# The opening of a two-layer decoder trunk: square sums moved to VectorE, a fourth gate block taken in, bank exchange and queue order rewritten

## The chip, the core and the metric

The kernel runs on one core of one Trainium2 chip. The metric is the device time of one execution in microseconds. The kernel before takes 2207.62 us (median of 3 runs, 2207.47 to 2208.49). In the profile PE is TensorE (PEld its weight loads), DVE is VectorE, ACT is ScalarE, POOL is GpSimd, and SP issues most DMAs. All arithmetic is float32; a product of two float32 matrices is made of three products of halves, high by high, high by low and low by high (fp32r), which is why every weight and every activation exists as a high and a low part.

## The reference

One sequence of 512 tokens, width 2048, passes two layers; the first is multi-scale retention with 8 heads, the second is latent attention. What matters here is how the first layer begins:

```python
def rmsnorm(x, g):
    xf = x.astype(jnp.float32)
    y = xf * lax.rsqrt(jnp.mean(xf * xf, axis=-1, keepdims=True) + EPS)
    return (y * g.astype(jnp.float32)).astype(x.dtype)

def reference(x, c, positions, ada_w, ada_b, norm_g, ret_w_in, ...):
    c_act = jax.nn.silu(c)
    for i in range(DEPTH):
        mod = (c_act @ ada_w[i] + ada_b[i])[:, None, :]
        shift, scale, gate = jnp.split(mod, 3, axis=-1)
        h = rmsnorm(x, norm_g[i]) * (1.0 + scale) + shift
        ...
def retention_branch(h, pos, w_in, gn_g, w_out):
    proj = h @ w_in
    q, k, v, g = jnp.split(proj, [RET_QK, 2 * RET_QK, 2 * RET_QK + RET_WIDTH], axis=-1)
```

So before any projection the kernel needs the sum of squares of each token (for the norm) and, for each block of 128 rows of h, two rows of matrix-vector products of silu(c) with ada_w (shift and scale). For each head of the first layer, q and k are 256 columns wide, v and the gate g are 512 columns wide.

## The kernel before, in words

Activations are kept transposed: hT has 16 blocks of 128 rows (128 of the width) by 512 tokens. The **opening** (lines 310 to 610) makes hT block by block and, while it does, already forms the products of head 0 with each block as it appears: q/k (four PSUM banks), v (four banks) and three of the four 128-column blocks of the gate g (three banks). A "unit" u is two blocks, 2u and 2u + 1; there are eight units.

The opening starts with x: eight tiles of two blocks are loaded, then squared (`square`, L456; ACT for even tiles, DVE for odd ones), folded to one block (`fold`, L466) and summed over the partitions by PE with a column of ones (`add_squares`, L469), 36 products of 128x1. `rsqrt` (L126) makes four columns of factors with one small DVE and one POOL instruction, `spread_one` (L499) spreads them over the partitions with a diagonal matrix and PE, and `normalise` (L504) multiplies x by them on DVE, straight from PSUM. silu(c) is spread over the partitions into c_all (L448).

For each block, two tiles of 1 MB of ada_w (`load_mod`, L336) are multiplied by c_all and summed along the row on DVE (`sum_mod`, L347, a 128x2048 instruction; for block 0 in two halves, L353). `make_first` (L363) turns the two sums into shift and scale on ACT and makes hT: the high part, a float copy (both ACT) and the low part (DVE). Weights are loaded by `first_load` (L319) and made into high (ACT) and low (DVE) parts.

v and q/k share one set of four PSUM banks (`acc`), so in each unit they are exchanged once: `swap` (L371) has ACT copy the four partial sums of the one out to SBUF and the four of the other back in. In an even unit PE forms q/k products for both blocks, then g, then (after the exchange) v; in an odd unit v first, then g, then q/k. `products` (L383) goes through a block by part and bank, `bank_products` (L396) through the second kind bank by bank.

The order on each engine is written out by hand: `queued` (L415) puts what it calls behind the last instruction written so far on ACT, DVE, PE and SP each. What is written without `queued` is bound only by its data and buffers. The weights and sums for unit u + 1 are prepared by `prepare_ahead` (L536, written ahead of unit u's products) and, for the odd block, by `prepare_behind` (L555, written behind the exchange). Buffers: four tiles for ada_w rows (`aw`), three for raw weights, three pairs for high and low weights, four `k4b` tiles that hold the squares first and the parts of g later, six `tmp` tiles.

In the last unit the rotary tables (`rotary_tables`, L251: a load of the positions, 17 DVE instructions, two Sin on ACT) are made: eight of its nine pieces are queued before the products, the rest behind the last exchange (L604); they are written to memory by POOL.

Behind the opening the work is a list of steps (L859 to L873), each with a load, a preparation (ACT and DVE), products and what follows them. First come two steps for block 3 of head 0's gate ("g03", 48 products), then for heads 1 to 5 eight steps of q/k and sixteen steps of v and g (`heads_steps`, L817, seven products instead of eight), for heads 6 and 7 only v and g. `sums` names the sums of hT (`form_sums`, L634) that a step forms beside its products; all eight must exist before head 1's v and g. `rows` says how many later modulation rows a step loads and sums beside. Stores of head 0's q/k and g are `keep_rows` (L616, called at L1903 to L1906).

Of the kernel before, what the change touches and what calls it, by code (L numbers as in the profile page):

```python
# [9 lines left out]
F32 = mybir.dt.float32  # L10
# [39 lines left out]
def hybrid_trunk_kernel(  # L50
# [247 lines left out]
    def qk_parts(h, u):  # L298
# [13 lines left out]
        "g": (3, lambda w, kt, b: (w_block(w, kt % 2, b), act_row(hT[kt]))),  # L312
# [6 lines left out]
    def first_load(kind, u):  # L319

        cn = 384 if kind == "g" else 512
# [25 lines left out]
    def sum_mod(kt, s):  # L347

        aw, n = mods[kt, s], 2 if kt == 0 else 1
        col = small(f"mc_{kt}_{s}", n)  # L350
        for j in range(n):
            cols = slice(j * D // n, (j + 1) * D // n)
            DVE.scalar_tensor_tensor(  # L353
                out=aw[:, cols], in0=aw[:, cols], scalar=1.0, in1=c_all[:, cols], op0=ALU.mult, op1=ALU.mult,
                accum_out=col[:, j : j + 1],
            )
        if n == 2:
            both = small(f"mc_{kt}_{s}b")
            DVE.tensor_add(both, col[:, 0:1], col[:, 1:2])
            col = both  # L360
        mods[kt, s] = col
# [9 lines left out]
    def swap(old, new):  # L371

        if old is not None:
            partial[old] = []
            for b, ps in enumerate(banks[old]):
                keep = l0p.tile([P, T], F32, tag="part", bufs=5, name=f"part_{old}_{len(loaded)}_{b}")
                ACT.copy(keep, ps)
                partial[old].append(keep)
        banks[new] = [acc(f"{new}0_{len(loaded)}_{b}") for b in range(4)]
        for b, keep in enumerate(partial.pop(new, ())):  # L380
            ACT.copy(banks[new][b], keep)
# [48 lines left out]
    def load_mods(kt):  # L430
        for s in range(2):
            mods[kt, s] = queued(load_mod, kt, s)
# [4 lines left out]
    mods[1, 0] = queued(load_mod, 1, 0)  # L437
    load_first("qk", 0)
    mods[1, 1] = queued(load_mod, 1, 1)
# [16 lines left out]
    def square(u, j=slice(0, 2)):  # L456
# [3 lines left out]
        o, i = sq[u][:, j, :], xT[u][:, j, :]  # L460
        if u % 2 and u < NU - 1:
            DVE.tensor_mul(o, i, i)
        else:
            ACT.activation(o, i, AF.Square)

    def fold(u):  # L466
        DVE.tensor_add(sq[u][:, 0, :], sq[u][:, 0, :], sq[u][:, 1, :])

    def add_squares(u, j=0):  # L469
        for t in range(NT):  # L470
            PE.matmul(
                x_sums[:, t : t + 1], sq[u][:, j, t * P : (t + 1) * P], crow, start=u + t == 0, stop=u + j == NU,
# [6 lines left out]
    for u in range(NU - 1):  # L479
        queued(square, u)  # L480
        if u < 4:
            queued(silu, u)
        if u % 2:
            queued(fold, u - 1)
            queued(fold, u)
            queued(add_squares, u - 1)
            queued(add_squares, u)
    for j in range(2):
        queued(square, NU - 1, j)
    queued(fold, NU - 2)  # L490
    queued(add_squares, NU - 1, 0)
    queued(add_squares, NU - 2)
    queued(add_squares, NU - 1, 1)
    r_col = queued(rsqrt, x_sums[:, 0:NT], NT, 1.0 / D, "x")
    POOL.dma_start(c_d, c_all[0:1, :])
    diag = tmp("x_diag")
    x_r = aux("x_r")

    def spread_one(t):  # L499
        cols = slice(t * P, (t + 1) * P)  # L500
        ACT.activation(diag[:, cols], ident, AF.Identity, scale=r_col[:, t : t + 1])
        PE.matmul(x_r[:, cols], ones, diag[:, cols], start=True, stop=True)

    def normalise(u, j=None):  # L504
        v = xT[u] if j is None else xT[u][:, j, :]
        r = x_r.unsqueeze(1).to_broadcast([P, 2, T]) if j is None else x_r
        DVE.tensor_mul(v, v, r)
# [5 lines left out]

    queued(scaled_bias)
    queued(sum_mod, 0, 0)
    for t in range(NT):
        queued(spread_one, t)
# [1663 lines left out]
```

## Time and profile before

| what | before |
|---|---|
| median of 3 runs | 2207.62 us (2207.47 to 2208.49) |
| span of the profiled execution | 2206.5 us |
| PE busy, instructions | 2162.7 us (98%), 10232 |
| DVE busy | 1562.9 us (71%) |
| ACT busy | 1014.6 us (46%) |
| bytes read from and written to memory | 395.42 and 43.00 MB, 199 GB/s over the span |
| first product of the opening | at 36.96 us |
| first product of head 1's q/k | at 188.16 us |

The profile is of one execution. A row of the timeline is: start, duration, engine, line, operation, out<-in with shapes, count of merged instructions, and in brackets the idle time of the engine before it and what released it. A row of the groups ends with busy time and mean ns of one, then idle time and releaser. A row of the waits is: total us, times, longest. Matmuls overlap, so the duration of one (0.39 us) is longer than the distance between two starts.

### The profile page before, as it was taken

The page shows a single profiled execution, that of the slowest core. Times are in us where ns is not written, and L with a number is a line of the kernel's source. Part 1 is how long each engine was busy: PE and PEld are TensorE (multiplying, and loading weights), DVE is VectorE, ACT ScalarE, POOL GpSimd, SP SyncE. Part 2 cuts the span into 40 slices and gives each one's busy share as a digit, 9 for nine tenths or more (in the row PEclk, how much of TensorE's full clock was granted, in tenths as well). Part 3 has the DMA queues.
Part 4 walks back from the last instruction along what each step waited for, and adds up shares of the span by engine and source line. Part 5 has one row for each costly group of instructions (what it writes and reads, how often), then busy time and mean ns, then how long its engine had stood idle before and what let it go on. Part 6 is the DMA issues. An engine that isn't in the chain of part 4 may idle for free.

```text
span 2206.5 us, 27730 instructions
## 1 busy us (share of the span) xinstructions
PE 2162.7 (98%) x10232; PEld 1806.3 (82%) x10232; DVE 1562.9 (71%) x2313; ACT 1014.6 (46%) x1547; POOL 101.9 (5%) x175
## 2 busy tenths in 40 slices
PE   7999999999999999999999999999999999999997
PEld 5777888888888877888888888888888889888887
DVE  5988866767676798866676776658877677766545
ACT  4764443434343444434343535434444366664443
POOL 0001000000001000000000000010000000000000
PEclk9999999999999999999999999999999999999999
DMA  7974686776868688674655556443458723235333
GB/s 302 354 275 164 195 283 223 232 251 198 277 198 268 210 283 276 203 242 141 209 189 179 191 171 215 155 157 120 145 199 293 275 90 94 85 105 180 111 104 134
DMA packets 207052, 440.26 MB, mean 200 GB/s; under 512 B 19346, under 2 KB 60338, under 8 KB 203074
## 3 DMA queue, kind: packets, MB, share of 16 engines
q1 hardware_dynamic: 194704, 399.30, 54.8%
q0 software_dynamic: 11920, 38.91, 4.5%
q8 instruction: 80, 1.31, 0.3%
q14 instruction: 58, 0.47, 0.1%
q10 hardware_dynamic: 290, 0.27, 0.0%
HBM read 395.42 MB, written 43.00 MB: 199 GB/s over the span
## 4 chain that ended last, share of the span: by engine, by line
PE 80%; DVE 8%; issue 4%; ACT 4%; DMA 2%; POOL 0%; SPq 0%; DVEq 0%; POOLq 0%; ACTq 0%
PE o L1191 13%; PE qk L163 4%; PE qk L162 4%; PE qk L161 4%; PE o L2047 4%; PE x L737 2%; PE y L737 2%; PE y L738 2%; PE y L736 2%; PE x L738 2%; PE s L737 2%; PE s L738 2%; PE x L736 2%; PE s L736 2%; PE g L161 2%
## 5 line engine op out<-in xcount | busy, mean ns | idle before, releaser
L1191 PE MATMUL o<-o_h,o_whi 128*128 128x512 f32 (+1 forms) x496 | 192.2, 388 | 0.0
L1191 PE MATMUL o<-o_h,o_wlo 128*128 128x512 f32 (+1 forms) x496 | 191.4, 386 | 0.0
L1191 PE MATMUL o<-o_l,o_whi 128*128 128x512 f32 (+1 forms) x496 | 191.3, 386 | 0.0
L163 PE MATMUL qk<-hT,qk_l 128*128 128x512 f32 x448 | 174.9, 390 | 0.4 <-DVE qk_l L136 0.4
L161 PE MATMUL qk<-hT,qk_h 128*128 128x512 f32 x448 | 174.5, 390 | 0.0
L162 PE MATMUL qk<-hT,qk_h 128*128 128x512 f32 x448 | 174.4, 389 | 0.0
L136 DVE TENSOR_TENSOR o_wlo<-o_r,o_whi 128x1024 fp32r<-128x1024 f32 x61 | 74.6, 1222 | 80.2 <-ACT o_whi L135 80.2
L136 DVE TENSOR_TENSOR qk_l<-qk_r,qk_h 128x1024 fp32r<-128x1024 f32 x56 | 68.1, 1223 | 62.4 <-ACT qk_h L135 62.1
L1191 PEld LDWEIGHTS o<-o_h,o_wlo 128*128 128x128 f32 x496 | 93.2, 188 | 18.8
L1191 PEld LDWEIGHTS o<-o_l,o_whi 128*128 128x128 f32 x496 | 93.2, 188 | 18.2
L1191 PEld LDWEIGHTS o<-o_h,o_whi 128*128 128x128 f32 x496 | 93.2, 188 | 18.2
L163 PEld LDWEIGHTS qk<-hT,qk_l 128*128 128x128 f32 x448 | 84.1, 188 | 19.4 <-DVE qk_l L136 2.1
L161 PEld LDWEIGHTS qk<-hT,qk_h 128*128 128x128 f32 x448 | 84.1, 188 | 17.5
L162 PEld LDWEIGHTS qk<-hT,qk_h 128*128 128x128 f32 x448 | 84.1, 188 | 17.5
L135 ACT CAST qk_h<-qk_r 128x1024 fp32r<-128x1024 f32 x56 | 57.8, 1049 | 85.6 <-PE qk L162 57.3
L161 PE MATMUL g<-h,g_h 128*128 128x512 f32 x232 | 90.6, 390 | 0.3 <-ACT g_h L135 0.3
L893 DVE SCALAR_TENSOR_TENSOR mod<-mod,c_bm 128x1024 f32<-128x1024 f32 x64 | 78.1, 1220 | 18.0 <-DMA mod<-in_ada_t_dram 18.0
L162 PE MATMUL g<-h,g_h 128*128 128x512 f32 x232 | 90.3, 389 | 0.0
L163 PE MATMUL g<-h,g_l 128*128 128x512 f32 x232 | 89.8, 389 | 0.0
L353 DVE SCALAR_TENSOR_TENSOR aw<-aw,c_all 128x2048 f32<-128x2048 f32 (+1 forms) x34 | 72.7, 2160 | 0.0
L135 ACT CAST o_whi<-o_r 128x1024 fp32r<-128x1024 f32 x61 | 63.5, 1052 | 19.6 <-issue 10.0
L136 DVE TENSOR_TENSOR o_w_lo<-o_w_raw,o_w_hi 128x1024 fp32r<-128x1024 f32 x32 | 38.9, 1220 | 39.4 <-ACT o_w_hi L135 39.4
(1260 smaller groups left out, 6014.3 us busy)
## 6 DMA issues: line engine op xcount, KB each, us to landing
mod<-in_ada_t_dram SPq DMA_DIRECT2D x128, 512.0 KB, 5.8
o_r<-in_ret_w_out_dram SPq DMA_DIRECT2D x64, 512.0 KB, 4.3
aw<-in_ada_t_dram SPq DMA_DIRECT2D x30, 1024.0 KB, 7.4
qk_r<-in_ret_w_in_dram SPq DMA_DIRECT2D x112, 256.0 KB, 3.9
g_r<-in_mla_w_in_dram SPq DMA_DIRECT2D x32, 512.0 KB, 4.6
o_w_raw<-in_mla_w_out_dram SPq DMA_DIRECT2D x32, 512.0 KB, 3.7
qk_d<-qk_st POOLq DMA_DIRECT2D x32, 256.0 KB, 3.5
qk_r<-qk_d SPq DMA_DIRECT2D x32, 256.0 KB, 6.2
```

The lines of the kernel that those rows point to most:

```text
L135: ACT.copy(hi, src)
L136: DVE.tensor_sub(lo, src, hi.bitcast(F32))
L161: PE.matmul(o, lhs[0], rhs[0], start=first and not seeded, stop=False, skip_group_check=seeded)
L162: PE.matmul(o, lhs[0], rhs[1], start=False, stop=False, skip_group_check=seeded)
L163: return PE.matmul(o, lhs[1], rhs[0], start=False, stop=last, skip_group_check=seeded)
L353: DVE.scalar_tensor_tensor(out=aw[:, cols], in0=aw[:, cols], scalar=1.0, in1=c_all[:, cols], op0=ALU.mult, op1=ALU.mult, accum_out=col[:, ...
L736: PE.matmul(banks[b], a[0], w[0], start=first, stop=False, skip_group_check=True)
L737: PE.matmul(banks[b], a[0], w[1], start=False, stop=False, skip_group_check=True)
L738: PE.matmul(banks[b], a[1], w[0], start=False, stop=True, skip_group_check=True)
L893: DVE.scalar_tensor_tensor(out=aw, in0=aw, scalar=1.0, in1=silu_c[j], op0=ALU.mult, op1=ALU.mult, accum_out=mc[:, j, b : b + 1],)
L1191: PE.matmul(o, w[i][:, ki, c0 + b * P : c0 + (b + 1) * P], a[j], start=first and i + j == 0, stop=last and i == 1, skip_group_check=True,)
L2047: PE.matmul(banks2[b][:, cols], w[0][i][:, 0, b * P : (b + 1) * P], o2_moving(w, u, cols)[j], start=u + i + j == 0, stop=u == KD - 1 and i ...
```

## The change

- **Squares**: ACT squares all tiles; DVE adds the squares of tiles 1 to 5 to those of tile 0 as they come (`gather`), then folds; tiles 6 and 7 are gathered into one block of their own. PE sums two blocks: 8 products instead of 36.
- **Factors**: two of the four diagonals are made on DVE; x_r is also copied to SBUF (`near`), and all but the first block are normalised from there. The sums for block 0 are queued by halves (`sum_part`) around the spread.
- **Gate**: all four blocks of head 0's gate are formed in the opening (four banks, 512 columns a load); the "g03" steps are gone.
- **Exchange**: `swap` is written bank by bank, out and back in turn; in units 1 to 7 `prepare` (one function instead of two) is written behind it, with the normalising and three sums ahead of the weights. The loads of a unit are ordered three ada_w tiles, weights, fourth ada_w tile, g, other weights. In the last unit `hand_over` copies v out and q/k in, bank by bank; all pieces of the rotary tables are written behind it, without `queued`.
- **Steps**: q/k of head 1, then q/k of head 2, then v and g of head 1, then v and g of head 2; from head 3 on as before. The sums of hT are spread over the sixteen q/k steps.

```diff
-        "g": (3, lambda w, kt, b: (w_block(w, kt % 2, b), act_row(hT[kt]))),
+        "g": (4, lambda w, kt, b: (w_block(w, kt % 2, b), act_row(hT[kt]))),
...
-        cn = 384 if kind == "g" else 512
+        cn = 512
...
+    def sum_part(kt, s, j):
+
+        if j == 0:
+            mods[kt, s] = mods[kt, s], small(f"mc_{kt}_{s}", 2)
+        aw, col = mods[kt, s]
+        cols = slice(j * D // 2, (j + 1) * D // 2)
+        DVE.scalar_tensor_tensor(
+            out=aw[:, cols], in0=aw[:, cols], scalar=1.0, in1=c_all[:, cols], op0=ALU.mult, op1=ALU.mult,
+            accum_out=col[:, j : j + 1],
+        )
+        if j == 1:
+            mods[kt, s] = small(f"mc_{kt}_{s}b")
+            DVE.tensor_add(mods[kt, s], col[:, 0:1], col[:, 1:2])
...
     def swap(old, new):
...
+        old_banks, back = banks.get(old, [None] * 4), partial.pop(new, [None] * 4)
+        partial[old], banks[new] = [], []
+        for b in range(4):
+            if old is not None:
                 keep = l0p.tile([P, T], F32, tag="part", bufs=5, name=f"part_{old}_{len(loaded)}_{b}")
-                ACT.copy(keep, ps)
+                ACT.copy(keep, old_banks[b])
                 partial[old].append(keep)
+            banks[new].append(acc(f"{new}0_{len(loaded)}_{b}"))
+            if back[b] is not None:
+                ACT.copy(banks[new][b], back[b])
+
+    def hand_over():
+
+        back, old_banks = partial.pop("qk"), banks["v"]
+        banks["qk"] = []
+        for b in range(4):
+            st = tmp(f"v0_st{b}")
+            ACT.copy(st, old_banks[b])
+            POOL.dma_start(v_d[b * P : (b + 1) * P, :], st)
+            banks["qk"].append(acc(f"qk0_{len(loaded)}_{b}"))
+            ACT.copy(banks["qk"][b], back[b])
...
+        ACT.activation(sq[u][:, j, :], xT[u][:, j, :], AF.Square)
+
+    def gather(to, u, j=None):
+        o, i = (sq[to], sq[u]) if j is None else (sq[to][:, 0, :], sq[u][:, j, :])
+        DVE.tensor_add(o, o, i)
...
+    silus = {1: 0, 2: 1, 4: 2, 5: 3}
+    for u in range(NU - 2):
         queued(square, u)
+        if u in silus:
+            queued(silu, silus[u])
+        if u > 0:
+            queued(gather, 0, u)
+    queued(square, NU - 2)
     for j in range(2):
         queued(square, NU - 1, j)
+    queued(gather, 0, 0, 1)
+    queued(add_squares, 0, True, False)
+    queued(gather, NU - 2, NU - 2, 1)
+    for j in range(2):
+        queued(gather, NU - 2, NU - 1, j)
+    queued(add_squares, NU - 2, False, True)
...
     queued(scaled_bias)
+    queued(sum_part, 0, 0, 0)
+    r_col = queued(rsqrt, x_sums[:, 0:NT], NT, 1.0 / D, "x")
...
     for t in range(NT):
         queued(spread_one, t)
+    low_v = queued(prepares["v", 0])
+    queued(sum_part, 0, 0, 1)
+    queued(sum_part, 0, 1, 0)
     queued(normalise, 0, 0)
+    queued(ACT.copy, near, x_r)
+    queued(sum_part, 0, 1, 1)
     low = queued(make_first, 0)
     queued(low_v)
+    low_g = queued(prepares["g", 0])
+    queued(low_g)
     queued(low)
...
     def load_unit(u):
         here, there = ("qk", "v") if u % 2 == 0 else ("v", "qk")
+        load_mods(2 * u)
+        load_mods(2 * u + 1, (0,))
         load_first(here, u)
+        load_mods(2 * u + 1, (1,))
         load_first("g", u)
         load_first(there, u)
...
+    def prepare(u):
         here, there = ("qk", "v") if u % 2 == 0 else ("v", "qk")
+        queued(normalise, u)
+        for s in range(2):
+            queued(sum_mod, 2 * u, s)
+        queued(sum_mod, 2 * u + 1, 0)
+        low_here = queued(prepares[here, u])
+        queued(low_here)
+        low = queued(make_first, 2 * u)
+        queued(sum_mod, 2 * u + 1, 1)
         queued(low)
+        low_g, low_there = (queued(prepares[kind, u]) for kind in ("g", there))
         low = queued(make_first, 2 * u + 1)
+        for fn in (low_g, low_there, low):
+            queued(fn)
...
     swap(None, "v")
     queued(products, "v", 0)
+    queued(sum_mod, 1, 0)
+    banks["g"] = [aux(f"g0_{b}") for b in range(4)]
     queued(products, "g", 0)
+    queued(queued(prepares["qk", 0]))
+    queued(normalise, 0, 1)
     queued(swap, "v", "qk")
+    queued(sum_mod, 1, 1)
     low = queued(make_first, 1)
+    queued(low)
     queued(products, "qk", 0)
-    prepare_ahead(1, low)
     queued(products, "qk", 1)
     queued(products, "g", 1)
     queued(swap, "qk", "v")
-    low = prepare_behind(1)
+    prepare(1)
     queued(products, "v", 1)
...
-            prepare_ahead(u + 1, low)
-        else:
-            queued(low)
-            for _ in range(8):
-                queued(next, tables)
...
         if more:
             queued(swap, here, there)
-            low = prepare_behind(u + 1)
+            prepare(u + 1)
         else:
+            queued(hand_over)
             for _ in tables:
                 pass
...
+    steps = qk_steps(1, sums=lambda u: {1: 0, 2: 1, 4: 2, 5: 3, 6: 4}.get(u))
+    steps += qk_steps(2, rows=lambda u: 1, sums=lambda u: {0: 5, 2: 6, 4: 7}.get(u))
     for h in range(1, RH):
+        if 2 < h < 6:
+            steps += qk_steps(h, rows=lambda u: 1)
         steps += heads_steps(h)
...
-    for b in range(3):
+    for b in range(4):
         queued(keep_rows, g0[b], g_d, b * P, f"g0_st{b}", AF.Silu, tmp)
```

`qk_steps` makes the same eight steps as the plain q/k steps before.

137 lines of the change are left out of this document (33 added, 104 removed).

## The prediction

> **What bounds the kernel now.** I read the windows first (columns: stretch, length, busy time and count of PE, PEld, DVE, ACT, POOL, then granted TensorE clock, DMA share, GB/s), cut at the first product of the opening and at the first product of the q/k step of head 1.
>
> ```profile
> 0.00:36.96 36.96, 24.69 (x88) 19.70 (x89) 15.22 (x26) 13.88 (x21) 4.36 (x11) 1.00 0.71 270
> 36.96:188.16 151.20, 138.52 (x577) 110.35 (x578) 127.02 (x135) 99.42 (x166) 7.03 (x13) 0.97 0.83 303
> 188.16:300.00 111.84, 111.29 (x483) 89.97 (x482) 93.75 (x133) 48.77 (x62) 2.67 (x5) 1.00 0.61 195
> ```
>
> From 188.16 on PE is idle for 0.55 us in 111.84: there only the number of matmuls counts, and the change leaves that number alone. All that can be won lies before 188.16. The middle stretch holds the opening's 16 x 33 = 528 products and the 48 of gate block 3: 576, and 577 are counted. What a product costs when nothing is waited for, and what a unit (two row blocks of h, 66 products) waits for, is in the timeline:
>
> ```profile
> 113.16 1.07 PE L392 MATMUL qk<-hT,qk_wlo 128*128 128x512 f32 x4
> ...
> 117.69 4.24 PE L392 MATMUL g<-hT,g_k4b 128*128 128x512 f32 x18
> 118.14 0.39 ACT L367 ACTIVATE a_col<-mc,bias,vcol 128x1 f32<-128x1 f32 x1 [4.44 <-DVE aw L353]
> ...
> 119.99 0.82 ACT L330 CAST g_k4b<-g_raw 128x768 fp32r<-128x768 f32 x1
> ...
> 121.67 0.57 ACT L377 COPY part_qk<-qk 128x512 f32<-128x512 f32 x1
> ...
> 122.91 0.50 PE L392 MATMUL v<-v_whi,hT 128*128 128x512 f32 x1 [0.98 <-ACT v L381]
> ```
>
> Between 113.16 and 117.69 PE starts 20 products: 0.2265 us each. So 576 need 130.5 us and got 151.20: **20.7 us are lost** between 36.96 and 188.16, beside the 36.96 before. The other rows show how a unit loses its part: ACT waits 4.44 us for a sum on DVE, then makes hT, casts g and the next weights, and only then reaches the bank exchange (121.67), so that PE has run out of g products and waits for the first bank at 122.91. One unit, and PE's waits grouped:
>
> ```profile
> 99.56:115.81 16.25, 15.27 (x68) 12.31 (x67) 14.51 (x15) 11.46 (x19) 0.00 (x0) 1.00 0.95 344
> ```
>
> ```profile
> PE v L392 <- ACT v L381: 8.9, 4, 5.9
> ...
> PE qk L392 <- ACT qk L381: 2.6, 3, 1.0
> ```
>
> A unit takes 16.25 us where 66 x 0.2265 = 14.95 are PE's: ACT and DVE waiting for each other set the pace, each of them with time to spare (DVE 14.51, ACT 11.46 busy). One exchange waited 5.9 us.
>
> **The start.** First the squares, their sums on PE, the factors, and the first product.
>
> ```profile
> 6.08 1.23 DVE L462 TENSOR_TENSOR x_sq<-x 128x1024 f32<-128x1024 f32 x1 [5.06 <-DMA x<-in_x_t_dram]
> ...
> 8.94 1.23 DVE L462 TENSOR_TENSOR x_sq<-x 128x1024 f32<-128x1024 f32 x1 [0.44 <-DMA x<-in_x_t_dram]
> ...
> 12.04 15.52 PE L471 MATMUL x_sums<-ones,x_sq 128*128 128x1 f32 x72
> ...
> 27.84 2.03 POOL L131 TENSOR_TENSOR x_r<-x_v,mhalf 128x4 f32<-128x4 f32 x1 [14.28 <-DVE bias L510]
> ...
> 30.36 2.08 PE L502 MATMUL x_r<-x_diag,ones 128*128 128x128 f32 x8 [2.80 <-ACT x_diag L501]
> ...
> 32.47 0.69 DVE L507 TENSOR_TENSOR x<-x,x_r 128x512 f32<-128x512 f32 x1 [2.15 <-PE x_r L502]
> ...
> 36.96 2.08 PE L392 MATMUL v<-v_whi,hT 128*128 128x512 f32 x4 [4.53 <-ACT hT L243]
> 38.83 1.79 PE L392 MATMUL v<-v_wlo,hT 128*128 128x512 f32 x4
> ```
>
> ```profile
> L353 DVE SCALAR_TENSOR_TENSOR aw<-aw,c_all 128x2048 f32<-128x2048 f32 x30 | 67.9, 2285 | 0.0
> L332 DVE TENSOR_TENSOR v_wlo<-v_raw,v_whi 128x1024 fp32r<-128x1024 f32 x8 | 9.8, 1224 | 1.3 <-ACT v_whi L330 1.2
> ...
> L507 DVE TENSOR_TENSOR x<-x,x_r 128x1024 f32<-128x1024 f32 x7 | 8.5, 1215 | 0.0
> L332 DVE TENSOR_TENSOR g_k4b<-g_raw,g_k4b 128x768 fp32r<-128x768 f32 x8 | 7.7, 958 | 0.0
> L353 DVE SCALAR_TENSOR_TENSOR aw<-aw,c_all 128x1024 f32<-128x1024 f32 x4 | 4.7, 1220 | 0.0
> L467 DVE TENSOR_TENSOR x_sq<-x_sq 128x512 f32<-128x512 f32 x7 | 4.6, 686 | 0.5 <-ACT x_sq L464 0.4
> ```
>
> ```profile
> L243 ACT ACTIVATE hT<-x,b_col,a_col 128x512 fp32r<-128x512 f32 x16 | 13.1, 816 | 0.5
> L381 ACT COPY v<-part_v 128x512 f32<-128x512 f32 x16 | 9.5, 591 | 0.5
> ...
> L330 ACT CAST v_whi<-v_raw 128x1024 fp32r<-128x1024 f32 x8 | 8.4, 1047 | 0.1
> ...
> L464 ACT ACTIVATE x_sq<-x 128x1024 f32<-128x1024 f32 x4 | 4.2, 1054 | 5.0 <-PE x_sums L471 3.6 <-DMA x<-in_x_t_dram 1.4
> ...
> L449 ACT ACT_TABLE_LOAD x1 | 1.3, 1283 | 0.0
> ```
>
> Before, 36 sums on PE (72 records, 0.216 us each) run without a gap from 12.04 to 27.56: they are the chain. After, 8 sums (16 records) remain, and DVE adds the squares instead. Tiles 1 and 3 of x are waited for until 6.08 and 8.94, so one comes every 1.43 us: tile 0 at 4.65, tile 7 at 14.7. ACT now makes all squares: eight tiles at 1.05 (8.4), four silus at 0.60 (as the copies of their shape; 2.4), one table load (1.28), 12.1 in all, from 4.65 to 16.7. DVE's adds of a whole tile (estimate 1.22, as the 128x1024 subtractions) follow each square with time to spare; behind the last square lies one add of 0.69, then 8 records on PE, 1.7: sums ready at 19.1. From there to the factors took 2.31 before (27.56 to 27.84 + 2.03 = 29.87), which gives 21.4; I take t0 = 22.0 (bounds 21 and 24: each DVE add may stand 0.7 in the way of the next). The half sum queued ahead of the factors on DVE needs the first half tile of modulation weights; at the pace of x it lands at 16.1, and its 1.22 us fit into PE's 1.7.
>
> Behind t0 DVE makes two diagonals (0.2 each, an estimate from the 0.69 of four times the width) and two half sums (2 x 1.22): t0 + 2.9, while PE's spread (2.57 after t0 before) is done. From normalise to the first product 4.49 us passed before (32.47 to 36.96) with two half sums between; now there is one, 1.15 less (1.22 and an overlap, below): 3.3. First product at t0 + 6.2 to 6.3 = **28.3 instead of 36.96: 8.7 gained.** The copy of x_r into near lies beside the half sum on ACT.
>
> **The first two units.** Counted from t0, by the rows above; neighbours on DVE overlap: a unit's rows above sum to 15.1 (4 x 2.29, 2 x 1.22, 1.22, 0.96, 2 x 0.69) and its busy time is 14.51, so I take some 0.07 off each. DVE's queue: v low 6.2, g low 9.2 (behind ACT's cast of g at 8.0, which stands behind both hT instructions), h0 low 9.9, sum (1,0) 12.1, q/k low 13.2, normalise 13.8, sum (1,1) 16.0; ACT: hT 1 17.3; DVE: h1 low 18.7, then the new prepare for unit 1: normalise 19.8, sums 22.0, 24.2, 26.4, weights low 27.6, sum 29.8, h2 low 30.4, g low 31.6, q/k low 32.7, h3 low 33.4. PE: v of block 0 starts at 6.3; its first eight run at the slow pace that the rows at 36.96 and 38.83 show (1.87 us from one four to the next), under the wait for h0 low at 9.9: end 10.8, 1.8 lost. g until 13.5, q/k of block 0 until 16.2, 1.1 lost until hT 1, then until 20.1, g 22.8, v of block 1 25.5; 1.5 lost until hT 2 (27.0), 1.7 until h2 low, 0.3 until h3 low. Sum 6.4 us lost, part of it the change's own: g low now stands ahead of h0 low. Do these gaps cost the clock as well?
>
> ```profile
> 10.00:20.00 10.00, 10.00 (x41) 8.30 (x39) 4.58 (x7) 4.52 (x7) 0.51 (x1) 1.00 1.02 396
> ...
> 50.00:60.00 10.00, 4.05 (x13) 2.53 (x12) 10.00 (x11) 6.78 (x11) 0.00 (x0) 0.70 1.03 396
> ```
>
> ```profile
> 57.79 0.79 PE L392 MATMUL v<-v_whi,hT 128*128 128x512 f32 x1 [5.93 <-ACT v L381]
> ```
>
> After 5.93 us idle the granted clock fell to 0.70; after 0.98 at 122.91 the products kept their pace. My gaps of 1.1 to 1.7 lie between: 0 to 6 us (three times the 1.9 that eight slow products, 2 x 1.87, cost more than 8 x 0.2265), nearest to the 0.98, so 0. The Trainium skill, TensorE: Matmul & The Clock Gate, Part 1, has the clock halved only after an idle window of about 3.4 us; by that rule too the term is 0, and the traces show no gap near that limit.
>
> **The later units.** PE now has 72 products, 16.31 us: v or q/k 5.45, g 5.45, the other 5.45. Measured from the unit's start T, by queue order: the exchange starts when the first bank is finished at T + 4.8 and its eight copies at 0.6 end at 9.7; its first bank is ready at 6.0 and needed at 10.9. prepare then stands behind it on ACT: cast of the next weights 10.8, hT even 12.3, cast of g 14.0, of the other 15.0, hT odd 16.4, its float copy 17.1. DVE: normalise and three sums by 9.2, weights low 12.0, fourth sum 14.3, h even low 15.0, g low 16.1, other low 17.2, h odd low 17.9. PE asks for hT even at 16.3, its low at 18.1, hT odd at 19.0, its low at 20.8. The smallest margin is 2.6 us, DVE's whole queue is 14.7 us, so **PE sets the unit at 16.31 and nothing more is lost** (that g grows by a third is hidden by this: 128x1024 instead of 128x768 costs DVE 0.27 a unit). The queue on SP has three modulation loads ahead of the next weights; each is issued when DVE frees its buffer, some 14 us ahead of its use.
>
> **The way out.** Head 1's q/k no longer has the 48 products of block 3 ahead of it. Copies of v, the return of q/k, qk0's and g0's stores: the eight copies of hand_over end at T + 9.7 of the last unit, and qk0's first three banks are finished and stored while PE works on. The rotary tables are what may be late:
>
> ```profile
> 163.05 0.43 DVE L257 CAST ret_sin<-ret_pi 128x512 f32<-128x512 int32 x1 [1.21 <-DMA ret_pi<-in_positions_dram]
> ...
> 173.48 0.63 ACT L279 ACTIVATE ret_sin<-ret_sin 128x512 f32<-128x512 f32 x1 [3.47 <-DVE ret_cos L277]
> ```
>
> ```profile
> ACT qk_st L619 <- DMA tables_d<-ret_cos: 1.6, 1, 1.6
> ```
>
> ```profile
> qk_d<-qk_st POOLq DMA_DIRECT2D x32, 256.0 KB, 3.5
> ```
>
> DVE and Sin took from 163.05 to beyond 174.1, and the store of qk0's second block waited for their way to memory. They are now written behind hand_over, without an edge that holds them there; DVE is free throughout the last unit. For the positions and the store I take the 3.5 us to landing that the last row gives for 256 KB. I take them as hidden and 0.7 us for the first split and its like; 11 us if they run behind the copies: T + 9.8, 3.5 for the positions, 10.4 for DVE, 1.3 for two Sin, 3.5 for the store make T + 28.5, against PE's need of that bank at T + 17.7.
>
> q/k of head 2 ahead of head 1's v and g moves eight steps and as many modulation loads; PE does the same work. Head 1's v and g are now followed by head 2's without q/k between, as those of heads 5, 6 and 7 were; two waits of that kind exist:
>
> ```profile
> PE x L737 <- DVE vg_01e_l L768: 1.0, 2, 0.5
> ```
>
> 0.5 us for one more such boundary, 0 to 1. The sums that these need get 16 steps instead of 10.
>
> **Sum.** Start 8.7; 20.7 lost before less 6.4 lost after, 14.3; less 0.7 and 0.5: 21.8 us. The profiled span 2206.5 becomes 2184.7; the median shown, 2207.62, lies 1.1 above that span, so **2186**.
>
> **Rivals.** (1) Tables late: up to 11 back, 2197; against it, nothing holds them there; for it, the place where they are written and the 1.6 us wait above. (2) Transfers set the pace. A unit moves 5.77 MB (four loads of 1.05 MB, three of 0.52), in 16.31 us 354 GB/s; the unit above had 344 at a share of 0.95. If 344 is all, a unit takes 16.8, six of them 3 us more; at 5 per cent less 17.7, 8 us: 2189 to 2194. Against it, no DVE sum waited for a load then. By the Trainium skill, DMA: Bandwidth & Descriptors, Specifications, HBM gives one core some 358 GB/s, which would leave 1 per cent; the stretch from 10 to 20 us, with 396, does not agree that this is a limit. (3) The opening stays at its ACT and DVE pace although the start is earlier (the change doesn't do what it says): h odd low comes 3 us later than I have it. Units then take 17.5 or so: 8.7 and 5 or 6 are left, 2194. (4) **Slower**: gaps that cost the clock in every unit. prepare now stands wholly behind the exchange. If its chain is longer than I have it by the margin and a gap large enough, every unit from 2 to 7 pays gap and slow pace: with 5.9 and 1.9, six units, 47 us, 25 more than is gained: 2233. Break-even is 3.6 us a unit. The rows place the limit between 0.98 and 5.93 us of idling; by the clock rule cited above a chain longer by 2.6 + 3.4 us would reach it. Against it: ACT and DVE would need 5 us more a unit than their rows sum to.
>
> **Chances.** Forecast 0.66, tables late 0.15, transfers 0.09, old pace 0.05, clock gaps 0.04; 0.01 for no change. All but the last two end over 0.2% (4.4 us, about what can be told from no change) under 2207.62: faster 0.95. The range: 2180 (t0 at 21, half of the 6.4 not lost, no loss on the way out) to 2197 (tables late).
>
> **What would show it.** The sums of squares are 16 records ending near 20; the first product at 28 to 29; PE waits of 1 to 2 us in the first two units and none on a bank from the third on; units 16.3 apart with PE as busy as after 188; the first product of head 1's q/k near 165 to 167. Wrong: units over 17; an ACT store waiting for tables_d; a clock under 1 behind the start; a wait for loads of aw.

## The result and the profile after

The changed kernel takes 2193.62 us (median of 4 runs, 2192.70 to 2194.78) against 2207.55 (4 runs, 2206.08 to 2208.49) beside it: a ratio of 0.9938, 95% interval 0.9924 to 0.9952. It is 0.6 per cent faster, and inside the range forecast (2180 to 2197), but 7.6 us above the forecast of 2186. The profiled span is 2192.7 instead of 2206.5.

The stretches of the kernel after, in the windows view (columns as in the prediction), cut at the first product of the opening (27.76), at g of the last unit (153.67), at the first product of head 1's q/k (173.15) and where head 1's v and g (263.02) and head 3's q/k begin; then the stretches of the kernel before from 188.16 on, cut at the same steps:

```profile
27.76:153.67 125.91, 123.30 (x528) 100.06 (x529) 111.29 (x107) 88.43 (x145) 0.00 (x0) 1.00 0.89 333
153.67:173.15 19.48, 11.04 (x49) 8.82 (x47) 10.39 (x18) 6.29 (x12) 3.30 (x6) 0.89 0.24 82
173.15:263.02 89.87, 89.87 (x384) 74.05 (x385) 66.40 (x104) 33.40 (x47) 7.77 (x15) 0.97 0.68 218
263.02:417.44 154.42, 154.42 (x674) 126.17 (x672) 121.53 (x153) 71.89 (x86) 7.03 (x14) 1.00 0.69 226
```

```profile
188.16:233.29 45.13, 44.68 (x194) 35.72 (x192) 40.22 (x68) 16.85 (x24) 0.54 (x1) 1.00 0.46 146
233.29:310.87 77.58, 77.48 (x338) 63.02 (x336) 60.20 (x75) 37.04 (x46) 4.05 (x8) 1.00 0.71 225
310.87:354.44 43.57, 43.57 (x194) 36.04 (x193) 26.07 (x35) 12.32 (x14) 3.74 (x8) 1.00 0.83 286
354.44:431.62 77.18, 77.18 (x337) 63.08 (x336) 57.43 (x73) 35.17 (x42) 2.72 (x6) 1.00 0.65 206
```

The first product comes 9.20 us earlier (36.96 to 27.76). From there to head 1's q/k it took 151.20 before and takes 145.39 now, a gain of 5.81 only. The q/k of heads 1 and 2 took 45.13 + 43.57 = 88.70 and take 89.87, 1.17 more; the v and g of these heads 77.58 + 77.18 = 154.76 and take 154.42, 0.34 less. Together 14.18; the rest of the span gives back 0.4. The second row of after is where the gain is missing: 49 products in 19.48 us, with PE busy for 11.04.

What PE waits for there, in the rows of ACT, DVE and PE in the timeline (bracket: idle time before, and the releaser):

```profile
153.19 1.07 ACT L396 COPY v_st<-v 128x512 f32<-128x512 f32 x2 [4.46 <-PE v L410]
...
156.37 0.36 ACTq L254 DMA_DIRECT2D ret_pi<-in_positions_dram  x1
...
160.00 0.43 DVE L257 CAST ret_sin<-ret_pi 128x512 f32<-128x512 int32 x1 [10.26 <-DMA ret_pi<-in_positions_dram]
...
169.71 0.69 DVE L277 SCALAR_TENSOR_TENSOR ret_cos<-ret_sin 128x512 f32<-128x512 f32 x1
...
170.43 0.63 ACT L279 ACTIVATE ret_sin<-ret_sin 128x512 f32<-128x512 f32 x1 [13.14 <-DVE ret_cos L277]
...
171.58 1.03 ACT L135 CAST qk_h<-qk_r 128x1024 fp32r<-128x1024 f32 x1
172.51 0.59 ACT L626 ACTIVATE qk_st<-qk 128x512 f32<-128x512 f32 x1
173.15 0.80 PE L161 MATMUL qk<-hT,qk_h 128*128 128x512 f32 x1 [8.44 <-ACT qk_st L626]
...
173.75 0.63 PE L162 MATMUL qk<-hT,qk_h 128*128 128x512 f32 x1
174.17 0.63 PE L163 MATMUL qk<-hT,qk_l 128*128 128x512 f32 x1
...
174.57 1.57 ACT L626 ACTIVATE qk_st<-qk 128x512 f32<-128x512 f32 x3 [1.47 <-DMA tables_d<-ret_cos]
```

Read from the top: ACT waits until 153.19 for PE to finish the first bank of v, and begins the eight copies of hand_over. The positions are loaded by ACT's own queue at 156.37, while the last copies run. (The buffer that they take does not hold the load back: by the order in which the `tmp` tiles are taken it was that of h_14f, which DVE read for the last time at 146.18.) DVE, idle for 10.26 us, begins the tables when they land at 160.00 and ends at 170.4. ACT, idle for 13.14 us, makes the two Sin, and only behind them come the first weight split of head 1 (171.58) and the first store of qk0 (172.51), which frees the bank that PE wants: 8.44 us of wait. The products after it start 0.42 to 0.43 us apart (173.75, 174.17) instead of 0.2265. The wait for tables_d itself (1.47 us ahead of 174.57) is ACT's and lies beside PE's work.

The start, in the timeline (PE's sums, DVE's last adds of squares, POOL's factors, PE's first products and its waits in the first two units):

```profile
16.12 1.86 PE L486 MATMUL x_sums<-ones,x_sq 128*128 128x1 f32 x8 [4.36 <-DVE x_sq L482]
16.77 1.49 DVE L482 TENSOR_TENSOR x_sq<-x_sq,x_sq 128x512 f32<-128x512 f32 x2
18.32 1.87 PE L486 MATMUL x_sums<-ones,x_sq 128*128 128x1 f32 x8 [0.33 <-DVE x_sq L482]
...
20.47 1.03 POOL L131 TENSOR_TENSOR x_r<-x_v,mhalf 128x4 f32<-128x4 f32 x1 [5.37 <-DVE x_v L129]
...
27.76 2.07 PE L410 MATMUL v<-v_whi,hT 128*128 128x512 f32 x4 [3.69 <-ACT hT L243]
...
38.69 1.21 PE L410 MATMUL qk<-hT,qk_whi 128*128 128x512 f32 x4 [0.40 <-ACT hT L243]
...
48.38 1.20 PE L410 MATMUL v<-v_whi,hT 128*128 128x512 f32 x4 [0.87 <-ACT hT L243]
...
51.84 2.10 PE L410 MATMUL v<-v_whi,hT 128*128 128x512 f32 x8 [1.35 <-DVE hT L246]
```

Sixteen records of sums end at 20.2, the factors are ready at 21.50, the first product starts 6.26 us later. Behind the first product the waits of 0.40, 0.87 and 1.35 us are the only ones; from 55.75, where g of unit 1 starts, to 153.67, where g of unit 7 starts, six units take 97.92 us, 16.32 each, with no wait of PE.

### The profile page after: what moved, and what is told of

It reads as the page before. It is cut to its first block, busy times and chain, and to the rows that moved or that the text cites. A ratio compares the mean times of both kernels' runs of the same rounds, so it can differ in the third digit from the quotient of the medians.

```text
span 2192.7 us, 27643 instructions
## 1 busy us (share of the span) xinstructions
PE 2149.2 (98%) x10176; PEld 1795.6 (82%) x10176; DVE 1563.2 (71%) x2312; ACT 1015.7 (46%) x1547; POOL 100.9 (5%) x175
## 4 chain that ended last, share of the span: by engine, by line
PE 85%; DVE 7%; issue 4%; ACT 2%; DMA 1%; POOL 0%; SPq 0%; DVEq 0%; POOLq 0%; ACTq 0%
PE o L1196 13%; PE qk L161 4%; PE qk L163 4%; PE qk L162 4%; PE o L2052 4%; PE x L744 2%; PE y L744 2%; PE y L745 2%; PE y L743 2%; PE x L745 2%; PE s L744 2%; PE s L745 2%; PE x L743 2%; PE s L743 2%; PE o L162 2%
## 5 line engine op out<-in xcount | busy, mean ns | idle before, releaser
L351 DVE SCALAR_TENSOR_TENSOR aw<-aw,c_all 128x2048 f32<-128x2048 f32 x30 | 67.5, 2286 | 0.0
```

The source lines that it names most:

```text
L351: DVE.scalar_tensor_tensor(out=aw, in0=aw, scalar=1.0, in1=c_all, op0=ALU.mult, op1=ALU.mult, accum_out=col,)
```

## The experiments

The theory after the result: the order on ACT (tables ahead of the first split and the first store) costs all of the missing time, and the rest of the prediction holds. The first two runs below move the tables. "Spread" is short for the kernel of tables_spread; the runs that are built on it have the tables where it has them.

**tables_spread** queues one piece of the tables with each unit, and the last three ahead of the last unit's products:

```diff
         if more:
             load_unit(u + 1)
+        else:
+            for _ in range(3):
+                queued(next, tables)
...
             prepare(u + 1)
+            queued(next, tables)
         else:
             queued(hand_over)
-            for _ in tables:
-                pass
```

> The changed kernel, with the rotary tables made piece by piece in the opening (one piece behind each unit's preparation, the last three ahead of the last unit's products) instead of behind the last exchange. Theory (tables): the 8.44 us that PE waits before head 1's q/k, and the slow clock behind it (13 products at 0.43 instead of 0.2265, 2.6 us), come from ACT's queue, where head 0's first q/k store and the first split stand behind the two Sin, which stand behind DVE's chain. Then the first product of head 1's q/k comes at 164 to 166 instead of 173.15, the clock stays at 1, and the time is 2193.6 - 11 = 2182.6 (2181.5 to 2184.5). Rival (banks): without block 3's steps between, q/k of head 1 must wait for head 0's banks whatever the tables do; then the time stays at 2193 and the wait at about 8.

Measured: **2182.29 us** (2181.77 to 2182.80), ratio 0.9883 (0.9869 to 0.9898): 11.3 us under the changed kernel. Its windows, cut at the first product, at head 1's q/k and at head 1's v and g:

```profile
27.57:164.39 136.82, 134.43 (x577) 109.21 (x577) 121.97 (x125) 95.96 (x158) 4.63 (x9) 1.00 0.86 325
164.39:251.43 87.04, 87.04 (x386) 72.07 (x384) 65.60 (x103) 32.43 (x45) 6.43 (x13) 1.00 0.66 214
251.43:405.85 154.42, 154.42 (x674) 126.18 (x673) 121.61 (x153) 72.06 (x86) 7.02 (x14) 1.00 0.70 226
```

and the rows that stand where the wait was:

```profile
153.58 0.63 ACT L279 ACTIVATE ret_sin<-ret_sin 128x512 f32<-128x512 f32 x1 [5.01 <-DVE ret_cos L277]
...
158.72 1.07 ACT L135 CAST qk_h<-qk_r 128x1024 fp32r<-128x1024 f32 x1
160.51 0.60 ACT L628 ACTIVATE qk_st<-qk 128x512 f32<-128x512 f32 x1 [0.72 <-PE qk L410]
```

The Sin now run ahead of the copies, the split at 158.72, and each store waits for PE instead of the other way round. PE goes on into head 1's q/k at 164.39 without a gap. So the opening is 14.38 us shorter than before (151.20 to 136.82), the two q/k 1.66 (88.70 to 87.04), v and g 0.34, and the start 9.39: 25.8 of the 26.0 us by which the span fell. The rival, that head 1's q/k must wait for head 0's banks wherever the tables stand, is refuted: the wait is gone.

**tables_last_unit** puts the pieces where the kernel before had them, eight ahead of the last unit's products:

```diff
         if more:
             load_unit(u + 1)
+        else:
+            for _ in range(8):
+                queued(next, tables)
```

> The changed kernel, with eight of the nine pieces of the tables queued ahead of the last unit's products, as the kernel before had them. Tables: the position load goes out at about 148.5 instead of 156.4, DVE's chain ends near 162.5 instead of 170.4, the two Sin, the first split and the first store end near 165; PE needs the bank at 164.7, so 1 to 2 us of waiting are left, too short for the clock: 2183 to 2185.5. Banks: 2193.

Measured: **2182.36 us** (2181.73 to 2183.65), ratio 0.9884 (0.9867 to 0.9900). The same as spread within the runs, and a little better than the 2183 to 2185.5 expected. The order on ACT, in its timeline:

```profile
161.35 0.63 ACT L279 ACTIVATE ret_sin<-ret_sin 128x512 f32<-128x512 f32 x1 [4.09 <-DVE ret_cos L277]
...
162.50 1.03 ACT L135 CAST qk_h<-qk_r 128x1024 fp32r<-128x1024 f32 x1
163.44 0.59 ACT L629 ACTIVATE qk_st<-qk 128x512 f32<-128x512 f32 x1
165.49 1.58 ACT L629 ACTIVATE qk_st<-qk 128x512 f32<-128x512 f32 x3 [1.46 <-DMA tables_d<-ret_cos]
```

The tables still stand ahead of the split and of the store, and the store of the second bank still waits for them; only everything comes 9.1 us earlier than after, just in time for PE, whose first product of head 1's q/k starts at 164.52. So it isn't the order alone that costs, but the order with the late load.

**squares_old** (spread, with the squares, folds and 36 sums of before put back) and **before_squares** (the kernel before with the new squares alone) price the start from both sides. The edit of squares_old, against the changed kernel:

```diff
-        ACT.activation(sq[u][:, j, :], xT[u][:, j, :], AF.Square)
+        if u % 2 and u < NU - 1:
+            DVE.tensor_mul(o, i, i)
+        else:
+            ACT.activation(o, i, AF.Square)
...
-            queued(gather, 0, u)
+            queued(fold, u - 1)
+            queued(fold, u)
+            queued(add_squares, u - 1)
+            queued(add_squares, u)
```

> tables_spread, with the squares, folds and 36 sums on PE of the kernel before. If the start counts in full: the sums end near 27.6 instead of 20.2, the first product comes 7 to 8 us later and so does everything: 2189.5 to 2190.5. If loads that go on during the later start give part of it back (the later units then find their data ready): 2184 to 2187.

> The kernel before, with the changed squares alone (all on ACT, gathered on DVE, 8 sums on PE). If the start adds by itself to whatever sets the later pace: first product 7 to 8 us earlier and 2199.5 to 2201. If the old opening's loads or its ACT and DVE chain take it back: 2203 to 2207.

Measured: squares_old **2189.64 us** (2188.91 to 2192.27), ratio 0.9919 (0.9904 to 0.9934), 7.4 over spread; before_squares **2200.30** (2199.54 to 2201.79), ratio 0.9970 (0.9958 to 0.9982), 7.1 under the kernel before beside it (2207.36). The squares are worth the same beside the old opening as beside the new one: the start adds, it isn't swallowed. The first product moves by 7.29 us with the squares alone (36.96 to 29.67), and by 1.92 without them (to 35.04 in squares_old): the second part lies behind the sums. DVE beside POOL's factors, first in before_squares (the old order behind the sums), then in squares_old (the new one):

```profile
20.47 1.22 DVE L353 SCALAR_TENSOR_TENSOR aw<-aw,c_all 128x1024 f32<-128x1024 f32 x1
...
20.55 2.03 POOL L131 TENSOR_TENSOR x_r<-x_v,mhalf 128x4 f32<-128x4 f32 x1 [5.36 <-DVE bias L508]
```

```profile
27.50 0.16 DVE L129 TENSOR_SCALAR x_v<-x_sums 128x4 f32<-128x4 f32 x1 [7.23 <-PE x_sums L489]
...
27.75 1.03 POOL L131 TENSOR_TENSOR x_r<-x_v,mhalf 128x4 f32<-128x4 f32 x1 [14.28 <-DVE x_v L129]
...
28.82 0.48 DVE L528 TENSOR_SCALAR x_diag<-ident,x_r 128x128 f32<-128x128 f32 x2 [1.15 <-POOL x_r L131]
```

With the old order a half sum of 1.22 us runs on DVE beside POOL's 128x4 factors, which take 2.03; with the new order DVE is idle from 27.66 to 28.82 and they take 1.03. That is 1.00 of the 1.92; another 0.84 is the way from the spread to the first product, one half sum shorter (PE waits 3.69 instead of 4.53 there).

**before_gate** is the kernel before with the fourth gate block, near and the new order of steps, but with the old squares, the old exchange, the old queue order and the old place of the tables; **gate_three** is spread with block 3 back in two steps of its own. The edit of gate_three against spread (before_gate has the changed kernel's side of these lines):

```diff
-        "g": (4, lambda w, kt, b: (w_block(w, kt % 2, b), act_row(hT[kt]))),
+        "g": (3, lambda w, kt, b: (w_block(w, kt % 2, b), act_row(hT[kt]))),
...
-        cn = 512
+        cn = 384 if kind == "g" else 512
...
+    steps = plain_steps(2, 8, ..., "g03", ...)
-    steps = qk_steps(1, ...)
+    steps += qk_steps(1, ...)
```

> The kernel before, with four gate blocks in its opening (x_r copied to SBUF for the bank) and the changed order of the steps, but the old squares, queue order and exchange. If the old pace is a chain of ACT and DVE in which a fourth block only adds its wider cast and subtraction (0.5 us): units of 16.6 to 16.8, 3 us longer in all, against 12.2 us of block 3's steps and 1.6 of crowded sums gone: 2196 to 2198. If the wait for the exchange stands behind PE's products, whatever their number: units of 16.31 + 1.4 = 17.7, 10 us longer in all: 2203 to 2205.

> tables_spread, with block 3 of the gate taken out of the opening again and its two steps put back behind it (48 products), all else as changed. If PE sets the pace of the units, 66 products take 15.0 us, DVE's queue 14.4 and ACT's about 12 just fit, the opening ends 10.5 to 10.9 us earlier and the 48 products take 10.9: 2182.5 to 2184.5, and the fourth block alone is worth nothing or little. If ACT and DVE still set a pace of 16.2, the steps cost their whole 10.9: 2192 to 2194.

Measured: before_gate **2198.56 us** (2196.64 to 2199.69), ratio 0.9961 (0.9946 to 0.9975), 8.8 under before (2207.36), 0.6 above the range of the first theory and far from the second; gate_three **2185.93** (2185.20 to 2186.88), ratio 0.9900 (0.9885 to 0.9915), 3.6 over spread. In before_gate, g starts at 70.09 in unit 1 and at 168.69 in unit 7: 16.43 a unit, where 72 products need 16.31. So the old exchange does not hold a unit of 72 products back; the old 16.25 for 66 was filled with the fourth block nearly for nothing. What the old order does cost is one wait in the second unit, in PE's rows:

```profile
58.54 0.79 PE L392 MATMUL v<-v_whi,hT 128*128 128x512 f32 x1 [5.46 <-ACT v L381]
```

With it, 33.08 us pass from the first product (37.01) to g of unit 1; in squares_old, which has the new order, 28.00 (35.04 to 63.04). The rewritten exchange and queue order are worth 5.1 us there, and 0.7 in the six units behind (98.60 us in before_gate, 97.94 in squares_old).

gate_three shows the other end. Its units of 66 products take 14.96 us three times (g at 55.05, 70.02, 84.97, 99.94), PE's own pace, and then 15.7 (to 146.97), with PE waiting for DVE once in each, 0.47, 0.36 and 0.40 us. The first of these waits, and the windows (PE, PEld, DVE and so on, as above) beside it:

```profile
111.90 2.14 PE L410 MATMUL v<-v_whi,hT 128*128 128x512 f32 x8 [0.47 <-DVE hT L246]
```

```profile
105.00:115.00 10.00, 9.53 (x42) 7.54 (x41) 10.00 (x12) 6.26 (x11) 0.00 (x0) 1.00 1.00 398
```

DVE is busy for all of the 10 us, PE for 9.53: in these units the exchange doesn't set the pace, DVE does. But part of DVE's work there comes from spread and not from the change: each of the last three units carries a piece of the rotary tables, two instructions of 0.69 us (at 114.37, 130.02 and 145.69). DVE is busy for 46.93 us from 99.94 to 146.97; without the three pieces, some 4.2 us, it would need 14.2 a unit, less than PE's 14.96. Of the 3.6 us that gate_three lies over spread, 2.1 are these three units and 1.3 a wait for the exchange of the last unit, which 18 products of g don't cover. So with the tables elsewhere the fourth block would be worth 1.5 us by this estimate, "nothing or little" as the first theory had it; no run shows that.

**steps_old** is spread with head 2's q/k back behind head 1's v and g, so that all eight sums of hT are given to the eight steps of head 1's q/k:

```diff
-    steps = qk_steps(1, sums=lambda u: {1: 0, 2: 1, 4: 2, 5: 3, 6: 4}.get(u))
-    steps += qk_steps(2, rows=lambda u: 1, sums=lambda u: {0: 5, 2: 6, 4: 7}.get(u))
+    steps = []
     for h in range(1, RH):
-        if 2 < h < 6:
-            steps += qk_steps(h, rows=lambda u: 1)
+        if h < 6:
+            steps += qk_steps(h, rows=lambda u, h=h: int(h > 1), sums=lambda u, h=h: u if h == 1 else None)
```

> tables_spread, with q/k of head 2 back behind v and g of head 1, so that all eight sums of hT are formed beside the eight q/k steps of head 1. If the order of the heads itself is worth nothing and only the room for the sums counts: a step then asks about 5.5 us of DVE (split 1.22, one set of sums 4.4) against PE's 5.45, and the eight steps take 2 to 4 us longer (before, six sums in them cost 1.6: 45.1 us against 43.6): 2184 to 2186.5. If the sums are hidden anyway: 2182.3 within 0.7. If the place of the steps matters by itself (boundary of heads 1 and 2, my 0.5): 2181.8.

Measured: **2188.13 us** (2187.43 to 2189.12), ratio 0.9914 (0.9897 to 0.9931): 5.8 over spread, in the expected direction and larger. The reason, in the timeline of DVE, ACT and PE at the step from q/k to v and g, and in the windows there:

```profile
207.18 1.29 DVE L136 TENSOR_TENSOR sums<-sums_f,sums 128x512 fp32r<-128x512 f32 x2 [0.23 <-ACT sums L135]
208.39 0.68 DVE L773 TENSOR_TENSOR vg_00e_r<-vg_00e_r 128x512 f32<-128x512 f32 x1
...
209.23 1.04 ACT L774 CAST vg_00e_h<-vg_00e_r 128x1024 fp32r<-128x1024 f32 x1 [1.57 <-DVE vg_00e_r L773]
210.69 1.05 ACT L779 CAST vg_00o_h<-vg_00o_r 128x1024 fp32r<-128x1024 f32 x1 [0.41 <-DVE vg_00o_r L776]
...
211.78 0.74 PE L745 MATMUL z<-vg_00o_h,hT 128*128 128x512 f32 x2 [3.06 <-ACT vg_00o_h L779]
...
212.91 1.28 DVE L646 TENSOR_TENSOR h_f<-hT 128x512 f32<-128x512 f32 x2
...
217.04 0.50 PE L745 MATMUL x<-vg_00e_h,hT 128*128 128x512 f32 x1 [0.68 <-ACT qk_st L628]
```

```profile
211.78:214.00 2.22, 2.17 (x7) 1.48 (x8) 2.22 (x3) 0.00 (x0) 0.00 (x0) 0.91 0.52 126
214.00:217.00 3.00, 2.36 (x6) 1.32 (x4) 2.71 (x7) 1.65 (x4) 0.00 (x0) 0.50 0.21 81
```

A step with its sums keeps DVE for 5.72 us (the sums of two steps in turn begin at 198.35 and 204.07), against 5.45 for PE, so DVE falls behind step by step. The seventh set of sums ends at 208.5, and only then DVE prepares the first weights of v and g, which ACT splits late (209.23, 210.69); the eighth set runs behind them, from 212.91. PE waits 3.06 us, and then the granted clock is 0.50 for some 3 us (1.00 again from 217). Head 1's q/k with the wait is 3.4 us longer than its products take, and the v and g behind it 2.7 longer than in spread (79.9 for 77.2), with a second wait of 0.68; the two make 6.1, so the place of head 2's q/k by itself shows no cost. The missing room cost more than the 2 to 4 us expected, which counted the q/k steps alone and no slow clock.

**warm** and **start_order** ask what sets the first two units. warm is spread with four unused products of 512 columns ahead of the first, and block 0's hT low ahead of g's low half on DVE; start_order has no such products, but that swap and the normalise of unit 1 ahead of block 1's hT low; **start_order_warm** has all three. The edits, warm's products first:

```diff
+    queued(warm, aux("warm"))
...
-    queued(low_g)
     queued(low)
+    queued(low_g)
...
-        queued(normalise, u)
+        if u > 1:
+            queued(normalise, u)
...
     low = queued(make_first, 1)
+    queued(normalise, 1)
     queued(low)
```

> tables_spread, with four products of 128x512 (ones by silu(c), their result unused) on PE between the spread of the factors and the first product, so that the clock is up when that comes, and h0's low part ahead of g's on DVE. The first eight products then take 1.8 us instead of 3.6. If DVE's queue sets the pace of the first two units (PE waits for hT 1, hT 2 and h2's low part anyway), nearly all of it is waited away again: 2181.8 to 2182.5. If the slow clock is on the path: 2180 to 2180.8.

> The version with the table pieces spread (2182.29), and in the first two units DVE's queue in another order: block 0's hT low goes ahead of the low half of the first g weights, and the normalise of unit 1 goes ahead of block 1's hT low, where DVE sat idle for 2.01 us. Theory (DVE's queue sets the first two units): block 2's hT comes some 1.5 us earlier (0.4 from the first, 1.15 from the second), the two waits of 0.88 and 1.38 shrink to 0.7 together, g of unit 1 starts near 54.0 instead of 55.6, 2180.8. Rival (PE's slow first products set them, or ACT's chain): no gain beyond 0.3 us, 2182.0 to 2182.5.

> The same new order of DVE's queue, and four more PE products of 512 columns ahead of the first product (their result goes nowhere), so that the clock is at its full pace when it comes. Theory (DVE's queue still sets the two units): 2180.5 to 2181.1, as without the four, with the time that they save shown again as waits for block 1's or block 2's hT. Rival (with DVE out of the way the 2.2 us of slow pace count): below 2180, down to 2179.3.

Measured: warm **2182.64 us** (2181.98 to 2182.85), ratio 0.9889 (0.9874 to 0.9904); start_order **2180.74** (2180.29 to 2181.76), ratio 0.9879 (0.9864 to 0.9894); start_order_warm **2181.11** (2179.56 to 2183.00), ratio 0.9881 (0.9865 to 0.9898). PE's first rows in warm, then its wait for block 2's hT low in start_order:

```profile
23.88 4.77 PE L542 MATMUL warm<-c_all,ones 128*128 128x512 f32 x8
28.09 1.48 PE L410 MATMUL v<-v_whi,hT 128*128 128x512 f32 x4
...
38.11 1.21 PE L410 MATMUL qk<-hT,qk_whi 128*128 128x512 f32 x4 [1.30 <-ACT hT L243]
```

```profile
51.01 2.36 PE L410 MATMUL v<-v_whi,hT 128*128 128x512 f32 x8 [0.65 <-DVE hT L246]
```

In warm the products are at full pace from 29.40 on, and most of what they save is given back as a wait of 1.30 us for block 1's hT: g of unit 1 starts 0.4 us earlier than in spread (55.17 for 55.56), and the time shows no gain, as the theory of DVE's queue had it. start_order shortens the wait for block 2's hT low from 1.38 to 0.65 and leaves the one of 0.88 for its high part, which ACT's eight copies of the exchange (40.96 to 45.9) hold up. From the first product to g of unit 1 it takes 27.38 us instead of 27.99: the trace shows 0.6 of the 1.5 expected. The median is 1.5 lower, but the other 0.9 stands nowhere near the edit (head 1's q/k starts 0.55 earlier, at 163.84 for 164.39), and the intervals of the two ratios overlap; I don't count it. With the four products as well (start_order_warm), g of unit 1 starts another 0.4 earlier, which the time can't show. start_order and spread lie 27.3 and 25.6 us under the kernel before beside each.

## Why the prediction was right, and where it was not

**The start**: 8.7 forecast, 9.20 measured. The sums ended at 20.2 instead of 19.1: two adds, not one, ran on DVE behind the last square (16.77 to 18.26). But the factors took 1.30 behind them instead of 2.31, as no half sum ran beside POOL any more. That two errors of one us cancelled is luck; t0 came at 21.5 for 22.0, the first product 6.26 later for 6.3.

**The first two units**: g of unit 1 was forecast 34.4 us after t0 and came 34.25 after; 6.25 us lost for 6.4. The waits fell on the operations named, each 0.3 to 0.7 shorter; the slow first products cost 2.2 instead of 1.8, and the products beside each wait were a little slower. The gaps up to 1.35 us cost no clock, the value taken.

**The units**: 16.31 forecast, 16.32 measured, set by PE. DVE is busy for 86.9 of the 97.92 us, 14.5 a unit for the forecast 14.7. In spread, with six pieces of the tables beside, it is busy for 96.3 of 97.95 and PE still doesn't wait, so the forecast margin was real.

**The way out**: this step failed. It read: "They are now written behind hand_over, without an edge that holds them there; DVE is free throughout the last unit", and "I take them as hidden and 0.7 us". Nothing in their data holds them, but their first instruction is a load that ACT issues, and in the trace it goes out at 156.37, with the last of the copies, which had themselves waited for PE until 153.19. Rival 1 had the price, 11 us, and the time, 2197 less what else went better. The runs put it at 11.3 (2193.62 less 2182.29): 8.44 of wait, and 2.6 for 13 products that start 0.43 apart. The rival's place was half right: it had the store of the second bank waiting for tables_d, and it was the split and the first store standing behind the two Sin. That 11 and 11.3 agree is luck in part: the rival's 11 was all waiting, with no slow clock in it. The prediction gave this case 0.15 although a row that it quotes, DVE waiting 1.21 us for the positions ahead of 163.05, shows a chain that starts with a load.

**The boundary and the sums**: 0.5 forecast for one more boundary between two v and g steps; none shows (154.42 for two, 77.2 each). "The sums that these need get 16 steps instead of 10" was costed at nothing. The crowded q/k of head 1 had cost 1.6 us before (45.13 against 43.57), and steps_old shows 5.8 in the time with only eight steps.

So the time lies inside the range because rival 1's time was its upper end; the likeliest case did not come. Spread, which has the tables out of the way as that case assumed, shows what it would have given, 25.8 us for the sum of 21.8: 0.7 more at the start, 0.1 in the opening, 1.7 from the sums' room, 0.8 at the boundary (0.3 gained for 0.5 lost) and 0.7 at the exit of spread. The 7.6 us by which 2186 was too low are 11.3 for the tables less the 3.7 by which spread ended below it.

**The other rivals**: transfers do not set the pace. No wait of PE in the later units is for a load, and the loads go faster than the 354 GB/s that a unit needs where there is room, in the windows of after:

```profile
55.00:65.00 10.00, 10.00 (x45) 8.26 (x45) 10.00 (x9) 9.49 (x16) 0.00 (x0) 1.00 1.04 412
```

The Trainium skill, DMA: Bandwidth & Descriptors, Specifications, gives one core some 358 GB/s; 412 goes beyond it, nearer to the 425 that the same page, in Bandwidth, has for large transfers of one core whose neighbour is idle. Rival 3, the old pace of ACT and DVE, is refuted by before_gate: even the old order carries 72 products at 16.43. Rival 4, gaps that cost the clock in each unit, did not come, as there are no gaps.

## What to carry to other kernels

An instruction without a data edge is still held by its place in its engine's stream; when a piece of work is moved, follow its first instruction, the load and the engine that issues it, and ask what stands behind its last one on that engine. A rival that is fully priced deserves a look for the row that decides it before it gets a small chance. Room for side work (here the sums of hT) counts as a term: crowding it into fewer steps shows up one step later, as late weights.

## What was not expected of the hardware

The granted clock around the wait of the kernel after, in its windows:

```profile
165.00:175.00 10.00, 1.85 (x4) 1.42 (x5) 6.38 (x9) 3.10 (x5) 1.62 (x3) 0.68 0.19 71
```

- With the wait of 8.44 us the granted clock reads 0.68 between 165 and 175, and behind it the products start 0.43 us apart for 5.7 us. With 3.06 us of idling in steps_old it reads 0.50 from 214 to 217, behind a stretch of 2.22 us that reads 0.91 (211.78 to 214). If that is 1.00 and then 0.50, it fell when PE had been at work again for 1.8 us. Waits up to 1.38 us left it at 1.00; what one between 1.38 and 3.06 does was not measured. The Trainium skill, TensorE: Matmul & The Clock Gate, Part 1, names an idle window of about 3.4 us; 8.44 and 1.38 lie on the sides that this gives, but 3.06 was enough here.
- The first 12 products of the opening are as slow (5.16 us from 27.57 to 32.73 in spread) with a granted clock that reads 1.00 there: that column doesn't show the slow start, the distance between products does.
- POOL's 128x4 factors took 2.03 us where a DVE half sum ran beside them and 1.03 where DVE was idle. The Trainium skill, SBUF — State Buffer, SBUF: two separate sides, says that a DVE instruction with two inputs in SBUF and a POOL one that reads SBUF exclude each other from a port pair that they share. That fits: in before_squares the half sum ended 1.14 us after POOL had begun, and the factors took 1.00 longer. No run moved that half sum alone.
